# The recurrence's token shift on VectorE alone, and another room for half of the read-out

## The chip, the cores and the metric

The kernel runs on one core of one Trainium2 chip. The metric is the time of one execution on the device, in microseconds (us). The core has five engines with a queue of instructions each: TensorE (PE; its weight loads are listed apart as PEld), VectorE (DVE), ScalarE (ACT), GpSimd (POOL) and SyncE (SP), which here issues all transfers. An engine takes its own instructions in order; engines wait for each other through semaphores. Matmuls write to banks of PSUM (128 partitions by 512 floats here); VectorE and ScalarE read these banks, and a bank can be written anew only when its readers are through.

## What is computed

A decoder layer on 1024 tokens of width 1024, in float32. A normalised input is multiplied by one wide matrix; its columns feed a windowed attention, an RWKV-7 recurrence with 8 heads of 64, and two gates. Their merged output goes through a projection, an MLP and an embedding gate. The part that matters here is the token shift ahead of the recurrence, and the recurrence's read-out:

```python
z = z + (token_shift(z) - z) * mu          # token_shift: z of the token before, 0 for the first
r, k, v, xw, xa, xg = jnp.split(z, RWKV_SPLITS, axis=-1)
...
_, y = lax.scan(step, state0, seq)
y = (y - mean) * lax.rsqrt(var + RWKV_GN_EPS)
y = y.reshape(B, S, RWKV_WIDTH) * ln_w.astype(f32) + ln_b.astype(f32)
...
y = (y + bonus.reshape(B, S, RWKV_WIDTH)) * g.astype(f32)
```

So each shifted tile is (1 - mu) times the product, plus mu times the product one token earlier.

## The kernel before, in words

Tokens lie along the free axis of the tiles of the recurrence, features along the partitions. The wide product is made in column blocks of 128 features, each in two halves of 512 tokens. One half is 24 matmuls into one bank: 8 slices of the width, and for each three products (`L310`, `L312`, `L314`), since a float32 operand is held as a rounded high part and a low remainder. The weights of a block are loaded by `wload`, rounded by ScalarE (`wh`) and the remainder made by GpSimd (`wl`, 128x1024).

The recurrence is worked in four units of 128 features (two heads). For each unit w, `add_rkv` makes the blocks of r, k and v; when a half is in its bank, `shift_half` takes it out of it and applies the token shift. While the recurrence runs, the dense halves alternate between two banks, z0 and z1 (`zbank`), so a half's first matmul waits until the half before the last has been taken out.

`shift_half` existed in two forms. The early form, used once for the small tiles `xw` and `xg`: ScalarE writes (1 - mu) times the bank to the tile (`omu` is its scale), and VectorE adds mu times the bank, shifted by one column, in one scalar_tensor_tensor; the first column of the second half comes from a kept column, `edge`. The other form, used for r, k and v (24 halves): ScalarE reads the bank twice, once for (1 - mu) times it, and once for mu times it into a tile `part`; GpSimd adds `part`, shifted, to the tile. `part` stands in the rooms of the tag `gst`, of which there are two; the same rooms stage the gate columns on their way to DRAM.

Per unit follow `elementwise` (decays, normalised keys; VectorE operations of 128x1024 elements: `AR`, `kk`, `BK`), `invert` (31 pairs of short VectorE steps, `pt` and `xy`), `fold_v` and `fold` (small matmuls), `scan` (14 steps, a small matmul `q` and a VectorE operation each), `read_out` (`y`), and `post`. `post` runs twice per unit, for the two token halves b = 0 and 1, one after the other: ScalarE squares the bank (`sq`) and copies it (`yc`), PE sums and transposes, VectorE makes `yc`, adds `bv` and multiplies into `og`, which is stored. Both halves used the one room `yc`, so the second half's copy had to wait for the first half's last reader.

The order of all this is set when the program is built. The class `Order` keeps an estimated clock; chains of the recurrence are recorded as they come due by it, and dense matmuls (the projections' blocks, among them the 16 gate blocks) fill PE's time between them. Each engine's estimated end moves with each operation recorded on it, and the steps of the inverse are put into VectorE's estimated idle time. So an operation that goes to another engine moves many others by some places. On the chip each engine then follows its recorded order.

Line numbers in the profile: most operations of VectorE, ScalarE and GpSimd go through one helper and are recorded under `L118` (held-back ones under `L115`), DMAs under `L137`; matmuls under `L293`, transposes under `L301`, and dense matmuls under `L310` to `L314`. So groups are told apart by the tiles' names.

## Time and profile before

| | us |
|---|---|
| median of 3 runs | 1758.35 |
| the three runs | 1755.95, 1758.35, 1758.49 |
| the profiled execution's own time | 1760.41 |
| its span, first to last instruction | 1758.6 |

The profile is of one execution. Of its span, roughly the first 50 us prepare the input, the recurrence lies between 50 and 525 us, attention up to about 830, merging and projection up to about 1050, and the MLP and the end take the rest. A row of the timeline gives start and duration in us, the engine, the line, the operation, output and inputs, shapes, and in brackets the idle time of that engine just before, with what ended it. A granted clock of 0.50 means that TensorE ran at half its full rate in that stretch.

### The profile page before, as it was taken

How to read it: one execution, taken by the hardware profiler on the slowest of the kernel's cores; microseconds unless marked ns; L12 is line 12 of the kernel's file. 1: busy time of each engine (PE TensorE's matmuls, PEld its weight loads, DVE VectorE, ACT ScalarE, POOL GpSimd, SP SyncE). 2: the span in 40 equal slices, each digit the busy share in tenths (PEclk: the TensorE clock that was granted, in tenths of full speed). 3: DMA queues.
4: the chain of work that ended last, by engine and by line, in shares of the span. 5: the costliest groups of instructions: out<-in, count | busy, mean ns of one | idle time of the engine just before them, and what ended most of it. 6: DMA issues, size and time to landing. Idle time of an engine off the chain costs nothing.

```text
span 1758.6 us, 26456 instructions
## 1 busy us (share of the span) xinstructions
PE 1731.2 (98%) x10132; PEld 1411.8 (80%) x10132; DVE 1102.0 (63%) x1878; ACT 751.6 (43%) x1377; POOL 639.5 (36%) x441
## 2 busy tenths in 40 slices
PE   9999999999999999999999998999999999999998
PEld 8787878887887877777888876888888888888887
DVE  6278876757635233444746652767788788787643
ACT  5833523342335343462534555333433443343354
POOL 1233111211212322322230346656656756752311
PEclk9999999999999999999999999999999999999999
DMA  4620121212342222232633386364464664567611
GB/s 164 213 96 28 58 90 56 80 36 81 113 141 92 67 60 61 84 138 103 212 108 126 108 326 248 124 224 160 145 234 179 204 227 163 203 223 271 224 49 48
DMA packets 99970, 244.78 MB, mean 139 GB/s; under 512 B 11394, under 2 KB 11778, under 8 KB 99331
## 3 DMA queue, kind: packets, MB, share of 16 engines
q1 hardware_dynamic: 99842, 243.08, 40.0%
q8 instruction: 80, 1.31, 0.3%
q14 instruction: 48, 0.39, 0.1%
HBM read 169.24 MB, written 67.11 MB: 134 GB/s over the span
## 4 chain that ended last, share of the span: by engine, by line
PE 82%; DVE 8%; ACT 4%; POOL 2%; issue 2%; DMA 2%; SPq 0%; DVEq 0%; ACTq 0%; POOLq 0%
PE z L314 15%; PE z L312 15%; PE z L310 15%; PE bk L310 8%; PE bk L314 8%; PE bk L312 8%; DVE tot L118 2%; DVE xy L118 1%; PE tp L301 1%; PE sc L293 1%; PE A L293 1%; PE y L293 1%; PE wr L293 1%; PE pt L301 1%; PE fq L293 1%
## 5 line engine op out<-in xcount | busy, mean ns | idle before, releaser
L310 PE MATMUL z<-uh,wh 128*128 128x512 f32 (+1 forms) x800 | 313.8, 392 | 2.5 <-ACT uh L118 1.3
L312 PE MATMUL z<-ul,wh 128*128 128x512 f32 (+1 forms) x800 | 314.3, 393 | 1.3 <-DVE ul L118 1.3
L314 PE MATMUL z<-uh,wl 128*128 128x512 f32 (+1 forms) x800 | 314.0, 392 | 1.2 <-POOL wl L118 1.1
L118 POOL TENSOR_TENSOR wl<-wr,wh 128x1024 fp32r<-128x1024 f32 (+1 forms) x56 | 133.8, 2390 | 469.4 <-ACT wh L118 461.7
L118 DVE TENSOR_TENSOR tot<-tot,bk 128x512 f32<-128x512 f32 x333 | 219.8, 683 | 82.2 <-PE bk L314 82.1
L310 PEld LDWEIGHTS z<-uh,wh 128*128 128x128 f32 x800 | 151.8, 190 | 33.6 <-issue 3.4
L314 PEld LDWEIGHTS z<-uh,wl 128*128 128x128 f32 x800 | 151.7, 190 | 32.8 <-issue 3.9
L312 PEld LDWEIGHTS z<-ul,wh 128*128 128x128 f32 x800 | 151.8, 190 | 32.0 <-issue 3.7
L118 ACT ACTIVATE wh<-wr 128x1024 fp32r<-128x1024 f32 (+2 forms) x94 | 81.1, 863 | 117.0 <-PE z L312 69.8
L118 ACT ACTIVATE hr<-hr 128x512 f32<-128x512 f32 x96 | 60.7, 632 | 133.4 <-DVE hr L118 131.9
L310 PE MATMUL bk<-duo 128*128 128x512 f32 x224 | 88.4, 395 | 0.4
L118 ACT ACTIVATE duo<-sum 128x512 fp32r<-128x512 f32 x64 | 39.7, 627 | 113.1 <-DVE sum L118 100.6
L312 PE MATMUL bk<-duo 128*128 128x512 f32 x224 | 87.7, 392 | 0.0
L314 PE MATMUL bk<-duo 128*128 128x512 f32 x224 | 87.6, 391 | 0.0
L310 PE MATMUL bk<-ws,duo 128*128 128x512 f32 x224 | 87.1, 389 | 0.0
L312 PE MATMUL bk<-ws,duo 128*128 128x512 f32 x224 | 87.1, 389 | 0.0
L314 PE MATMUL bk<-ws,duo 128*128 128x512 f32 x224 | 87.1, 389 | 0.0
L310 PE MATMUL z<-f,wh 128*128 128x512 f32 x212 | 83.1, 392 | 3.5 <-ACT pa L118 3.5
L314 PE MATMUL z<-f,wh 128*128 128x512 f32 x212 | 83.4, 393 | 1.3 <-POOL wh L118 1.3
L118 POOL TENSOR_TENSOR wh<-wr,wh 128x512 fp32r<-128x512 f32 x38 | 54.5, 1436 | 81.3 <-ACT wh L118 81.3
L312 PE MATMUL z<-f,wh 128*128 128x512 f32 x212 | 83.0, 391 | 0.0
L118 DVE TENSOR_TENSOR hr<-hr,z 128x512 f32<-128x512 f32 x80 | 54.6, 682 | 23.4 <-PE z L314 23.3
(372 smaller groups left out, 4052.4 us busy)
## 6 DMA issues: line engine op xcount, KB each, us to landing
wr<-in_wz_dram SPq DMA_DIRECT2D x48, 512.0 KB, 3.8
w2r<-in_w_ff_dram SPq DMA_DIRECT2D x34, 512.0 KB, 4.6
bs<-duo SPq DMA_DIRECT2D x32, 512.0 KB, 4.9
duo<-bs SPq DMA_DIRECT2D x32, 512.0 KB, 4.2
wr<-in_wff_dram SPq DMA_DIRECT2D x56, 256.0 KB, 3.6
hr<-p1scr SPq DMA_DIRECT2D x48, 256.0 KB, 4.0
xt<-in_x_dram SPq DMA_DIRECT2D x16, 512.0 KB, 3.8
gscr<-gst SPq DMA_DIRECT2D x32, 256.0 KB, 2.2
```

Of the source, the lines that this page charges most:

```text
L118: return f(*a, **kw)
L293: PE.matmul(out_, a, b, start=start, stop=stop)
L301: PE.transpose(out_, a, ident if idn is None else idn)
L310: PE.matmul(ps, ah, bh, start=start and i == 0, stop=False, skip_group_check=not start)
L312: PE.matmul(ps, ah, bl, start=False, stop=False, skip_group_check=not start)
L314: PE.matmul(ps, al, bh, start=False, stop=i == n - 1, skip_group_check=not start)
```

## The change

`shift_half` keeps the early form only and uses it for r, k and v too. The tile `part`, its 24 ScalarE copies and all of GpSimd's adds are gone; VectorE reads the bank a second time instead. In `post`, the second half's `yc` moves to one of the two `gst` rooms that `part` no longer uses.

```diff
-    def shift_half(dst, ps, h, mu, om, edge, early=False):
+    def shift_half(dst, ps, h, mu, om, edge):
         lo, hi = h * 512, h * 512 + 512
         S.activation(dst[:, lo:hi], ps, AF.Copy, scale=om)
-        if early:
-            if h == 0:
-                V.tensor_copy(edge, ps[:, 511:512])
-            else:
-                V.scalar_tensor_tensor(dst[:, lo:lo + 1], edge, mu, dst[:, lo:lo + 1], op0=OP.mult, op1=OP.add)
-            V.scalar_tensor_tensor(dst[:, lo + 1:hi], ps[:, 0:511], mu, dst[:, lo + 1:hi],
-                                   op0=OP.mult, op1=OP.add)
-            return
-        part = rtile([128, 512], "part", "gst")
-        S.activation(part, ps, AF.Copy, scale=mu)
         if h == 0:
-            G.tensor_copy(edge, part[:, 511:512])
+            V.tensor_copy(edge, ps[:, 511:512])
         else:
-            G.tensor_tensor(dst[:, lo:lo + 1], edge, dst[:, lo:lo + 1], OP.add)
-        G.tensor_tensor(dst[:, lo + 1:hi], part[:, 0:511], dst[:, lo + 1:hi], OP.add)
+            V.scalar_tensor_tensor(dst[:, lo:lo + 1], edge, mu, dst[:, lo:lo + 1], op0=OP.mult, op1=OP.add)
+        V.scalar_tensor_tensor(dst[:, lo + 1:hi], ps[:, 0:511], mu, dst[:, lo + 1:hi], op0=OP.mult, op1=OP.add)
...
-            shift_half(t, ps, h, pr[:, c], omu[:, c], edges[:, n:n + 1], True)
+            shift_half(t, ps, h, pr[:, c], omu[:, c], edges[:, n:n + 1])
...
-        yc = rtile([128, 512], "yc", "yc")
+        yc = rtile([128, 512], "yc", ("yc", "gst")[b])
```

Since the order is recorded by estimates, the instructions of all engines move up to the first projection. VectorE's queue in the first unit's `elementwise`, after the change (each row one instruction, or several alike; `v<-z` is the new operation on a half of v in its bank `z`):

```order
L118 TENSOR_TENSOR BK<-a,En 128x16x64
L118 COPY edge<-z 128x1
L118 SCALAR_TENSOR_TENSOR v<-z,pr,v 128x511
L115 COPY wc<-Ep 128x16
L115 TENSOR_TENSOR AR<-r,Ep 128x1024
L118 SCALAR_TENSOR_TENSOR kk<-k,pr,bc 128x512 x2
L118 SCALAR_TENSOR_TENSOR AR<-kk,Ep 128x16x63
L118 TENSOR_SCALAR AR<-kk 128x16
L118 TENSOR_TENSOR BK<-BK,En 128x16x64
L118 SCALAR_TENSOR_TENSOR v<-edge,pr,v 128x1
L118 SCALAR_TENSOR_TENSOR v<-z,pr,v 128x511
L118 TENSOR_TENSOR BK<-BK,kk 128x16x64
```

Before, the rows without `z` and `edge` stood there in the same order, and GpSimd made v beside them. The second half of v now stands behind the whole block of six operations from `AR<-r,Ep` to `BK<-BK,En`. In the second unit these rows stand in the same order, with steps of the inverse (`pt`, `xy`) ahead of and behind them.

ScalarE's queue in the second unit, from the exponentials to the gate columns, before:

```order
L118 ACTIVATE En<-Ep 128x1024
L118 ACTIVATE v<-z,omu 128x512
L118 ACTIVATE part<-z,pr 128x512
L115 ACTIVATE Ep<-Ep 128x1024
L118 ACTIVATE v<-z,omu 128x512
L118 ACTIVATE part<-z,pr 128x512
L118 ACTIVATE wh<-wr 128x1024
L118 ACTIVATE gst<-z 128x512 x2
```

and in the same place after the change:

```order
L118 ACTIVATE En<-Ep 128x1024
L118 ACTIVATE wh<-wr 128x1024
L118 ACTIVATE v<-z,omu 128x512
L115 ACTIVATE Ep<-Ep 128x1024
L118 ACTIVATE v<-z,omu 128x512
L118 ACTIVATE wh<-wr 128x1024
L118 ACTIVATE gst<-z 128x512 x2
```

Both `part` copies are gone, and the rounding `wh` of a block's weights, which stood ahead of the reciprocal norms, now stands between `En` and the first half of v.

## The prediction

> **What bounds the kernel now.** First the page: the span, and the busy time by engine.

> ```profile
> span 1758.6 us, 26456 instructions
> PE 1731.2 (98%) x10132; PEld 1411.8 (80%) x10132; DVE 1102.0 (63%) x1878; ACT 751.6 (43%) x1377; POOL 639.5 (36%) x441
> ```

> TensorE is busy for 98% of the span. It executes the same matmuls after the change, so nothing is won by work taken from ScalarE or GpSimd as such; only two things can move the end: the idle time of PE, 27.4 us in all, and the time it runs at a lower granted clock. So next come PE's own waits, by what ended them (total, times, longest; the rows that touch the changed lines).

> ```profile
> PE q L293 <- DVE AR L118: 1.9, 2, 1.0
> PE z L310 <- ACT part L118: 1.2, 1, 1.2
> PE A L293 <- ACT yc L118: 1.0, 1, 1.0
> ```

> The tiles of the change appear there twice, once each: the scaled copy `part` costs PE 1.2 us, the read-out tile `yc` 1.0 us. Third, the granted clock. The stretches below are (duration, PE busy, PEld, DVE, ACT, then PEclk); I chose the borders at the clock's own changes.

> ```profile
> 262.33:265.75 3.42, 2.70 (x65) 2.58 (x66) 3.33 (x5) 0.98 (x2) 0.00 (x0) 1.00 0.30 106
> 265.75:272.57 6.82, 6.82 (x44) 5.22 (x41) 3.42 (x3) 1.85 (x3) 3.39 (x3) 0.50 0.18 65
> 351.08:354.49 3.41, 3.41 (x17) 2.27 (x16) 3.41 (x2) 2.11 (x2) 0.00 (x0) 0.50 0.83 217
> 361.32:364.73 3.41, 3.41 (x49) 3.32 (x47) 1.39 (x3) 3.36 (x6) 0.00 (x0) 1.00 0.02 5
> 364.73:368.15 3.42, 3.42 (x12) 2.60 (x9) 1.25 (x2) 3.38 (x8) 0.00 (x0) 0.50 0.00 0
> ```

> Three times in the recurrence the clock is halved, for 6.82, 3.41 and 3.42 us, which costs half of that: 3.4, 1.7 and 1.7 us, 6.8 us together. The first halving follows the stretch in which PE waits for `yc`. [...] So I count the halvings as something that the order of small matmuls can bring or take, and not as a fixed cost.

> **The change part by part.** Every token-shift half had two reads of the bank by ScalarE and an add by GpSimd. The view of the tile `part` and, for the form that replaces it, of `xw` and `edges`, where the kernel already has it (instructions, min/median/max in ns):

> ```profile
> L118 ACT ACTIVATE part<-z,pr x24: 673/682/697, 55.2 to 373.6; 128x512 f32<-128x512 f32 x24
> L118 POOL TENSOR_TENSOR r<-part,r x8: 1086/1090/1306, 57.6 to 334.5; 128x511 f32<-128x511 f32 x8
> L118 DVE SCALAR_TENSOR_TENSOR xw<-z,pr,xw x2: 737/740/742, 37.3 to 44.6; 128x511 f32<-128x511 f32 x2
> L118 DVE COPY edges<-z x2: 147/148/150, 37.2 to 38.3; 128x1 f32<-128x1 f32 x2
> L118 DVE SCALAR_TENSOR_TENSOR xg<-edges,pr,xg x1: 220/220/220, 48.4 to 48.4; 128x1 f32<-128x1 f32 x1
> ```

> ScalarE loses 24 x 0.682 = 16.4 us, GpSimd 24 x 1.09 = 26.2 us and its small edge operations. VectorE gains 24 x 0.740 + 12 x 0.148 + 12 x 0.220 = 22.2 us between 54 and 375 us. None of these is a term by itself. What counts is that **the bank is now given back by VectorE**, behind whatever stands in VectorE's queue. Two banks alternate here, so a bank must be free again when the next half's 24 matmuls are through. These rows of ScalarE time that: each copy starts when a half ends.

> ```profile
> 149.41 0.50 PE L310 MATMUL z<-uh,wh 128*128 128x512 f32 x1 [1.21 <-ACT part L118]
> 155.30 0.60 ACT L118 ACTIVATE gst<-z 128x512 f32<-128x512 f32 x1 [2.89 <-PE z L314]
> 160.72 0.60 ACT L118 ACTIVATE gst<-z 128x512 f32<-128x512 f32 x1 [4.82 <-PE z L314]
> ```

> A half takes 160.72 - 155.30 = 5.42 us. That is the cover. For most of the 24 it is enough, since VectorE has no block of long operations ahead: for r and k the new operations stand between the short steps of the inverse, and I cost them at nothing. If the cover were gone, each would cost its 0.96 us.

> *First unit, v, second half.* Here the new operations stand behind a block. VectorE's timeline of that block before the change, and GpSimd's split beside it:

> ```profile
> 90.90 1.40 DVE L118 SCALAR_TENSOR_TENSOR kk<-k,pr,bc 128x512 f32<-128x512 f32 x2
> 92.33 1.97 DVE L118 SCALAR_TENSOR_TENSOR AR<-kk,Ep 128x1008 f32<-128x1008 f32 x1
> 94.23 2.37 DVE L118 TENSOR_SCALAR AR<-kk 128x16 f32<-128x16 f32 x1
> 96.50 1.21 DVE L118 TENSOR_TENSOR BK<-BK,En 128x1024 f32<-128x1024 f32 x1
> 93.20 3.36 POOL L118 TENSOR_TENSOR wl<-wr,wh 128x1024 fp32r<-128x1024 f32 x1
> 90.80 0.69 ACT L118 ACTIVATE v<-z,omu 128x512 f32<-128x512 f32 x1 [1.33 <-PE z L314]
> 96.32 0.60 ACT L118 ACTIVATE gst<-z 128x512 f32<-128x512 f32 x1 [3.30 <-PE z L314]
> ```

> The v half ended at 90.8, the next at 96.3, and there PE wants the bank back. PE has the same matmuls ahead of that point in the new order. VectorE is through with `BK<-BK,En` at 96.50 + 1.21 = 97.7; then 0.22 + 0.74, less two overlaps of 0.1 such as between the rows at 94.23 and 96.50, give 98.5. That is a wait of 98.5 - 96.3 = **2.2 us**. If GpSimd's split did not stand in the way, the 128x16 operation would take 0.17 us (a row of the second unit, below) instead of 2.37, and the wait would be nothing. The bounds are 0 and 2.2; I take 2.2, because the split follows the same `wh` in the new order and the rows are those of this very place.

> *Second unit, v.* VectorE's block in that place:

> ```profile
> 151.92 1.21 DVE L115 TENSOR_TENSOR AR<-r,Ep 128x1024 f32<-128x1024 f32 x1
> 153.05 1.39 DVE L118 SCALAR_TENSOR_TENSOR kk<-k,pr,bc 128x512 f32<-128x512 f32 x2
> 154.48 3.17 DVE L118 SCALAR_TENSOR_TENSOR AR<-kk,Ep 128x1008 f32<-128x1008 f32 x1
> 157.57 0.17 DVE L118 TENSOR_SCALAR AR<-kk 128x16 f32<-128x16 f32 x1
> 157.65 1.22 DVE L118 TENSOR_TENSOR BK<-BK,En 128x1024 f32<-128x1024 f32 x1
> 148.11 0.67 ACT L118 ACTIVATE v<-z,omu 128x512 f32<-128x512 f32 x1
> 151.34 1.07 ACT L118 ACTIVATE wh<-wr 128x1024 fp32r<-128x1024 f32 x1
> 144.08 0.17 DVE L118 TENSOR_SCALAR rn<-hs 128x16 f32<-128x16 f32 x1
> 249.09 1.86 DVE L118 SCALAR_TENSOR_TENSOR AR<-kk,Ep 128x1008 f32<-128x1008 f32 x1
> ```

> For the first half PE waited until 149.41 behind `part`. In the new order a weight's rounding `wh` (1.07 us) stands ahead of that half's ScalarE copy, and 0.148 + 0.740 of VectorE behind it, so by the old clock times the release would be 148.11 + 1.07 + 0.67 + 0.89 = 150.7, 1.3 us later. Against that, the normalisation that everything here hangs on reads its bank at 144.08, behind a backlog of the inverse's steps, and the new order puts fewer of them in front. Bounds: 1.2 us won to 1.3 us lost. I take **0**, the middle, as no row decides.

> For the second half VectorE has 1.21 + 1.39 + 1.86 + 0.17 + 1.22 + 0.22 + 0.74 = 6.8 us, from the first half's release to the second's, against a cover of 5.42 us: a wait of 1.4 us; with the slowed 3.17 instead of 1.86, 2.7 us. I take **1.4**, because a split that used to be beside this operation has moved to the front of the first half.

> *The read-out.* `yc` of the second half gets one of the two `gst` rooms. Before, it waited for the first half's last reader:

> ```profile
> 263.05 0.49 PE L293 MATMUL A<-AR,BK 64*128 64x128 f32 x4 [1.05 <-ACT yc L118]
> ```

> That wait goes: **-1.05**. Next in line for the same matmul is ScalarE's square, which stands just ahead of the copy. What the room costs: a gate's copy two places behind `yc` has to wait for the read-out's last product. In the new order one read-out (first unit) is followed by the next-but-one gate copy only after the fold's copies, another (third unit) after two copies of the inverse. Nothing to 2 us, on ScalarE; I take 0, since PE's other bank covers 5.42 us of it.

> VectorE's added 22.2 us push each unit's inverse back; the new order lets PE do dense work there, taken from the gate columns (the first fold starts 46 dense matmuls later). That costs nothing as long as dense work is left, and 25 dense matmuls, 5.6 us, still stand behind the last attention product (73 before). The scan's steps may wait for VectorE as in the first waits row (two, 1.9 us); bounds -1.9 to +3.8 (four halves of 0.96 us fall among scan steps); I take 0.

> **Sum** against the profiled execution's own 1760.41 us: +2.2 + 0 + 1.4 - 1.05 = +2.55. The profiled execution is 2.06 us above the median 1758.35, so the forecast is 1758.35 + 2.55 = **1760.9 us**, no difference that a measurement tells: I call 0.2%, 3.5 us, the limit of that.

> **The rivals.**

> *Faster.* The yc wait goes and with it the half clock behind it: -1.05 - 3.4. VectorE also gets back what GpSimd's adds took from it.

> ```profile
> 124.56 1.31 POOL L118 TENSOR_TENSOR r<-part,r 128x511 f32<-128x511 f32 x1 [0.32 <-ACT part L118]
> 124.56 0.35 DVE L118 TENSOR_TENSOR pt<-xy,Mp 64x192 f32<-64x192 f32 x1
> 124.94 1.13 DVE L118 TENSOR_TENSOR xy<-xy,pt 64x192 f32<-64x192 f32 x1
> 246.37 3.51 POOL L118 TENSOR_TENSOR wl<-wr,wh 128x1024 fp32r<-128x1024 f32 x1 [14.72 <-ACT wh L118]
> 247.65 1.41 DVE L118 SCALAR_TENSOR_TENSOR kk<-k,pr,bc 128x512 f32<-128x512 f32 x2
> ```

> Beside such an add a step of 192 elements took 1.13 us instead of its neighbour's 0.35. With the adds gone the banks come back in time, and the 1.21 us goes as well: -5.7, 1752.7 us. For it: the halving follows the yc wait directly. Against it: the splits of the weights remain, and they are the longer GpSimd operations. [...] Chance 0.23.

> *Slower.* The mechanism is the bank release: PE's first matmul of the gate half that follows v stands and waits. With both waits at their long end and the first half not won back it is 2.2 + 1.3 + 2.7 - 1.05 = 5.15, and a wait of this length in a stretch makes the next one half as fast, as 262.33:265.75 did with 2.70 us busy of 3.42: 1.7 us once: +6.85, 1765.2 us. It decides from the point where VectorE's release comes more than 5.42 us after the half's end. A third fold with less dense work between its small matmuls, as the new order has it, adds another 1.7. Chance 0.32.

> *No effect at all.* ScalarE and GpSimd were covered, VectorE's operations are, too, and only yc's 1.05 goes: 1757.3 us, inside the same 0.2%. Chance 0.12, and 0.33 for my sum.

> **How the numbers follow.** The two cases within 0.2% hold 0.45, faster 0.23, slower 0.32. The range reaches from the faster rival to the slower one with another halving: 1752 to 1768.

> **What would show it.** Right: PE waits of 1 to 3 us ended by "DVE v" at about 97 and 155 us, no wait for `part` or `yc`; the DVE busy time up by some 15 to 22 us, POOL down by about 30. Wrong: no wait ended by a shifted tile at all; or a wait for `r` or `k`; or another count of half-clock stretches than three in the recurrence, which moves the time by 1.7 us each; or ScalarE waiting for a `gst` room.

## The result and the profile after

The changed kernel takes 1753.6 us (median of 20 runs, 1751.6 to 1757.8), the kernel before 1758.42 us beside it (20 runs, 1755.0 to 1763.85). The ratio is 0.9971, 95% interval 0.9962 to 0.998: **faster by 0.3%**, 5 us. The prediction was 1760.9 us, no difference; the measured time lies in its range of 1752 to 1768, near the end that the faster rival gave. A second comparison on another chip gave 0.9957 (0.9941 to 0.9973).

The page of the changed kernel, span and busy times:

```profile
span 1753.7 us, 26435 instructions
PE 1727.1 (98%) x10132; PEld 1409.0 (80%) x10132; DVE 1108.6 (63%) x1926; ACT 736.9 (42%) x1353; POOL 606.0 (35%) x393
```

The span is 4.9 us shorter, and PE is busy 4.1 us less with the same 10132 matmuls: its idle time went from 27.4 to 26.6 us only. Less the time that the whole span lost at half clock (10.9 us before, 5.8 us after), PE's busy time is 1720.4 us before and 1721.3 us after, so what it gained is clock. PE's waits, the rows that answer to those shown of before (total, times, longest):

```profile
PE z L310 <- DVE v L118: 3.2, 2, 2.7
PE q L293 <- DVE AR L118: 1.7, 4, 0.6
```

The waits for `part` (1.2 us) and `yc` (1.0 us) are gone, and two waits for `v` from VectorE have come, 3.2 us together. By these rows alone the kernel would be a microsecond slower. So I look at the stretches around the clock (duration, PE busy, PEld, DVE, ACT, POOL, granted clock); the first row is nearly the whole recurrence:

```profile
56.00:525.00 469.00, 462.88 (x4038) 380.54 (x4037) 321.85 (x615) 168.58 (x253) 78.41 (x41) 1.00 0.26 91
148.00:151.42 3.42, 0.72 (x5) 0.33 (x4) 3.39 (x7) 1.63 (x2) 1.34 (x2) 1.00 0.00 0
151.42:154.83 3.41, 3.41 (x9) 2.67 (x10) 3.41 (x4) 0.00 (x0) 1.27 (x1) 0.50 0.00 0
274.30:277.71 3.41, 3.41 (x80) 2.93 (x80) 3.31 (x4) 0.59 (x1) 0.00 (x0) 1.00 0.34 132
```

The same row of the kernel before:

```profile
56.00:525.00 469.00, 461.70 (x4018) 378.80 (x4018) 314.23 (x571) 183.98 (x278) 110.32 (x88) 0.99 0.27 92
```

In the recurrence there is now one half clock, 3.41 us at 151.4 us, behind the longer wait for `v`; before there were three, 13.66 us in all. That is 5.1 us of full-clock time (13.66 - 3.41, halved), as much as the whole difference of the two spans. The fold in the second unit (274.30: 80 matmuls, most of them 32x32) is at full clock; before, the stretch that held it (262.33, 65 matmuls, with the `yc` wait) was followed by 6.82 us at half clock.

This is one profile of each kernel, and a second one of each, taken for the experiments, divides the gain otherwise: PE's idle time in the whole span falls from 27.3 to 24.8 us, and the time lost at half clock only from 7.6 to 6.2 us. Over all executions on that chip the mean granted clock is 0.9950 before and 0.9967 after, which is 3.0 us of a difference of 7 us. So the clock is one part of the gain, and PE's waits are the other.

The two waits for `v`, in the timeline of the changed kernel:

```profile
92.71 3.32 POOL L118 TENSOR_TENSOR wl<-wr,wh 128x1024 fp32r<-128x1024 f32 x1 [8.96 <-ACT wh L118]
93.70 2.35 DVE L118 SCALAR_TENSOR_TENSOR v<-edge,pr,v 128x1 f32<-128x1 f32 x1
95.97 0.73 DVE L118 SCALAR_TENSOR_TENSOR v<-z,pr,v 128x511 f32<-128x511 f32 x1
96.85 0.47 PE L310 MATMUL z<-uh,wh 128*128 128x512 f32 x1 [0.46 <-DVE v L118]
...
145.87 2.39 POOL L118 TENSOR_TENSOR wl<-wr,wh 128x1024 fp32r<-128x1024 f32 x1 [14.44 <-ACT wh L118]
145.88 2.65 DVE L118 TENSOR_TENSOR xy<-xy,pt 64x247 f32<-64x247 f32 x1
148.46 1.21 DVE L118 TENSOR_TENSOR BK<-a,En 128x1024 f32<-128x1024 f32 x1
149.59 0.39 DVE L118 TENSOR_TENSOR pt<-xy,Mp 64x240 f32<-64x240 f32 x1
150.02 0.40 DVE L118 TENSOR_TENSOR xy<-xy,pt 64x240 f32<-64x240 f32 x1
150.41 0.73 DVE L118 SCALAR_TENSOR_TENSOR v<-z,pr,v 128x511 f32<-128x511 f32 x1
151.29 0.66 PE L310 MATMUL z<-uh,wh 128*128 128x512 f32 x1 [2.70 <-DVE v L118]
```

In the first unit a one-element add took 2.35 us beside GpSimd's split, but VectorE's block had begun early enough: 0.46 us of wait. In the second unit a step of the inverse took 2.65 us beside a split (its neighbours take 0.4), and behind it stood 1.21 + 0.39 + 0.40 us of other work before the first half of `v` could be taken out: 2.70 us. The large operation itself, fed from the bank, took 0.73 us in both places, in the second unit beside a split that began at 150.34 us.

### The profile page after: what moved, and what is told of

The parts are those of the page before. It is cut to its first block, busy times and chain, and to the rows that moved or that the text cites. A ratio compares the mean times of both kernels' runs of the same rounds, so it can differ in the third digit from the quotient of the medians.

```text
span 1753.7 us, 26435 instructions
## 1 busy us (share of the span) xinstructions
PE 1727.1 (98%) x10132; PEld 1409.0 (80%) x10132; DVE 1108.6 (63%) x1926; ACT 736.9 (42%) x1353; POOL 606.0 (35%) x393
## 3 DMA queue, kind: packets, MB, share of 16 engines
q8 instruction: 80, 1.31, 0.3%
## 4 chain that ended last, share of the span: by engine, by line
PE 80%; DVE 7%; ACT 4%; DMA 4%; issue 2%; POOL 2%; SPq 1%; DVEq 0%; ACTq 0%; POOLq 0%
PE z L310 15%; PE z L314 15%; PE z L312 15%; PE bk L310 8%; PE bk L314 8%; PE bk L312 8%; PE tp L301 1%; PE sc L293 1%; PE A L293 1%; PE po L293 1%; PE pt L301 1%; PE wr L293 1%; PE fq L293 1%; DVE duo L118 1%; POOL wl L118 1%
## 5 line engine op out<-in xcount | busy, mean ns | idle before, releaser
L118 POOL TENSOR_TENSOR wl<-wr,wh 128x1024 fp32r<-128x1024 f32 (+1 forms) x56 | 133.3, 2382 | 589.8 <-ACT wh L118 584.4
L310 PE MATMUL z<-uh,wh 128*128 128x512 f32 (+1 forms) x800 | 313.4, 392 | 4.0 <-DVE v L118 3.2
L314 PE MATMUL z<-uh,wl 128*128 128x512 f32 (+1 forms) x800 | 312.9, 391 | 0.7 <-POOL wl L118 0.7
L118 DVE TENSOR_TENSOR tot<-tot,bk 128x512 f32<-128x512 f32 x333 | 219.6, 681 | 82.3 <-PE bk L314 82.1
L310 PEld LDWEIGHTS z<-uh,wh 128*128 128x128 f32 x800 | 151.0, 189 | 36.0 <-issue 4.9
L314 PEld LDWEIGHTS z<-uh,wl 128*128 128x128 f32 x800 | 151.1, 189 | 31.8 <-issue 3.7
L118 ACT ACTIVATE wh<-wr 128x1024 fp32r<-128x1024 f32 (+2 forms) x94 | 81.0, 862 | 119.5 <-PE z L312 65.9
L118 ACT ACTIVATE hr<-hr 128x512 f32<-128x512 f32 x96 | 60.7, 632 | 134.8 <-DVE hr L118 133.3
L310 PE MATMUL bk<-duo 128*128 128x512 f32 x224 | 88.4, 395 | 0.3
L314 PE MATMUL bk<-duo 128*128 128x512 f32 x224 | 87.5, 391 | 0.0
L314 PE MATMUL bk<-ws,duo 128*128 128x512 f32 x224 | 87.1, 389 | 0.0
L310 PE MATMUL bk<-ws,duo 128*128 128x512 f32 x224 | 87.1, 389 | 0.0
L118 ACT ACTIVATE duo<-sum 128x512 fp32r<-128x512 f32 x64 | 39.7, 628 | 112.4 <-DVE sum L118 100.5
L310 PE MATMUL z<-f,wh 128*128 128x512 f32 x212 | 83.1, 392 | 3.5 <-ACT pa L118 3.5
L314 PE MATMUL z<-f,wh 128*128 128x512 f32 x212 | 83.4, 393 | 1.3 <-POOL wh L118 1.3
L118 POOL TENSOR_TENSOR wh<-wr,wh 128x512 fp32r<-128x512 f32 x38 | 54.5, 1437 | 81.2 <-ACT wh L118 81.2
L118 DVE TENSOR_TENSOR hr<-hr,z 128x512 f32<-128x512 f32 x80 | 54.5, 681 | 23.4 <-PE z L314 23.3
```

The lines of the kernel that those rows point to most:

```text
L118: return f(*a, **kw)
L310: PE.matmul(ps, ah, bh, start=start and i == 0, stop=False, skip_group_check=not start)
L314: PE.matmul(ps, al, bh, start=False, stop=i == n - 1, skip_group_check=not start)
```

## The experiments

Three theories stood against each other: the gain is in the *order* of the matmuls and the clock that it is granted (A), in the *work* and the waits that it brought (B: ScalarE's and GpSimd's parts of the shift no longer in anyone's way), or in the new *room* alone (C). Since the planner sets the order by the work that it is told of, the work and the order can be parted: an inserted engine that does nothing takes the calls that only the planner is to see, and the real operations are issued beside it.

### The room alone

The kernel before with one line changed; every compute engine has the same instructions in the same order.

```diff
-        yc = rtile([128, 512], "yc", "yc")
+        yc = rtile([128, 512], "yc", ("yc", "gst")[b])
```

> Only the room of yc changes: the second half's read-out gets one of the gst rooms, the shift stays on ScalarE and GpSimd, and every compute engine has the same instructions in the same order as before. Theory A (the gain of the changed kernel is clock: fewer half-clock stretches in the recurrence, brought by another order of the small matmuls): the 1.05 us wait of PE for yc goes; the half clock at 265.7 us, which followed that wait, may go with it or stay, since no order has changed: between -1 us (1757.4) and -4.5 us (1753.9). Theory B (the gain is PE's waits for part and yc, 1.2 + 1.05 us): -1.0 us, 1757.4, three half-clock stretches in the recurrence as before. Theory C (the whole gain sits in the room alone): 0.997, about 1753.6.

Measured: 0.9983 (0.9973 to 0.9993), -3.0 us. More than the wait alone (theory B) and less than the whole (theory C). In its profile the wait for `yc` is gone and so is the half clock behind it; one of 3.41 us at 352 us is left. The recurrence:

```profile
56.00:525.00 469.00, 461.81 (x4044) 379.24 (x4044) 320.25 (x582) 187.45 (x285) 113.46 (x89) 1.00 0.28 93
```

### The changed kernel with the old room

```diff
-        yc = rtile([128, 512], "yc", ("yc", "gst")[b])
+        yc = rtile([128, 512], "yc", "yc")
```

> The changed kernel with yc back in its single room; the order on every engine is that of the changed kernel. Theory A (order of the matmuls sets the half-clock stretches): one half-clock stretch in the recurrence instead of three, as in the changed kernel, or one more if the yc wait is back and brings it: 0.997 to 0.998, 1753.6 to 1756.3. Theory B (waits): the yc wait is back, 1754.7. Theory C (the room): 1758.4, as before.

Measured: 0.9984 (0.9973 to 0.9994); the changed kernel has 0.9971 and 0.9957. The order on every engine is that of the changed kernel, so the stretch at 274 us can be laid beside the one above. First the timeline of PE with the old room, then the stretches:

```profile
274.35 0.39 PE L310 MATMUL z<-uh,wh 128*128 128x512 f32 x1
274.66 0.48 PE L293 MATMUL A<-AR,BK 64*128 64x128 f32 x2
276.19 1.16 PE L293 MATMUL A<-AR,BK 64*128 64x128 f32 x14 [1.04 <-ACT yc L118]
277.28 2.57 PE L293 MATMUL tq<-TN,TM 32*32 32x32 f32 x64
279.78 0.80 PE L312 MATMUL z<-ul,wh 128*128 128x512 f32 x1
```

```profile
275.44:278.85 3.41, 2.66 (x63) 2.54 (x64) 3.32 (x5) 0.94 (x2) 0.00 (x0) 1.00 0.27 100
278.85:285.68 6.83, 6.83 (x46) 5.29 (x42) 3.49 (x3) 1.90 (x3) 3.40 (x3) 0.50 0.22 68
```

With the old room the wait of 1.04 us is back in the stretch that holds the fold, and behind it 6.83 us at half clock, 3.4 us lost. So the room takes away 1.05 us of wait *and* the half clock behind it, in either order.

The same matmuls in the changed kernel:

```profile
274.34 0.39 PE L310 MATMUL z<-uh,wh 128*128 128x512 f32 x1
274.66 1.16 PE L293 MATMUL A<-AR,BK 64*128 64x128 f32 x16
275.75 2.21 PE L293 MATMUL tq<-TN,TM 32*32 32x32 f32 x64
277.89 0.50 PE L312 MATMUL z<-ul,wh 128*128 128x512 f32 x1
```

From the end of the last dense matmul (`z`) to the start of the next it is 5.0 us with the wait and 3.2 us without it. A whole stretch of 3.41 us, as at 275.44, can stand without a dense matmul only in the first. That is how a wait of 1 us can bring a half clock; it is read from these rows and was not tried by itself.

### The new work in the old order, and the old work in the new one

The first has VectorE's shift and the new room, but the planner is told of the old work; TensorE's matmuls stand exactly as in the kernel before. The second has ScalarE's and GpSimd's shift and the new room, but TensorE's matmuls exactly as in the changed kernel.

```diff
+        S.eng, G.eng = NoOp(), NoOp()
         part = rtile([128, 512], "part", "gst")
         S.activation(part, ps, AF.Copy, scale=mu)
...
+        S.eng, G.eng = nc.scalar, nc.gpsimd
...
+        nc.vector.scalar_tensor_tensor(dst[:, lo + 1:hi], ps[:, 0:511], mu, dst[:, lo + 1:hi], op0=OP.mult, op1=OP.add)
```

```diff
+            V.eng = NoOp()
...
         V.scalar_tensor_tensor(dst[:, lo + 1:hi], ps[:, 0:511], mu, dst[:, lo + 1:hi], op0=OP.mult, op1=OP.add)
+        V.eng = nc.vector
...
+        part = rtile([128, 512], "part", "gst")
+        nc.scalar.activation(part, ps, AF.Copy, scale=mu)
...
+        nc.gpsimd.tensor_tensor(dst[:, lo + 1:hi], part[:, 0:511], dst[:, lo + 1:hi], OP.add)
```

> VectorE makes the second term, and yc has the new room, but the order is that of the kernel before: TensorE has the same matmuls in the same order as before, and VectorE's added operations stand where the shift stood. Theory A (order): no gain, 1758.4 or up to 2.2 us more from the bank waits; the half clocks at 351 and 364.7 us, which are far from any shift, are still there. Theory B (work: ScalarE's copy of the bank and GpSimd's adds in VectorE's way): 0.997, 1753.6.

> ScalarE and GpSimd make the second term as before, and yc has the new room, but TensorE's matmuls, VectorE's and ScalarE's remaining operations stand in the order of the changed kernel. Theory A (order): 0.997, 1753.6, less the two bank waits behind VectorE (3.2 us together) plus a wait for part of about 1 us: 1750 to 1754, with at most one half-clock stretch in the recurrence. Theory B (work): 1.000, 1757 to 1758.4, three half-clock stretches.

Measured: new work, old order 1.0011 (1.0 to 1.0022); old work, new order 0.9959 (0.9944 to 0.9975). Theory B falls on both, and theory C falls with the room alone, which gives only 3.0 of the 5 us. With the same room and the old order, VectorE's work costs 1.0011 - 0.9983 = 0.0028, 4.9 us, and the intervals are apart. Its waits for `v` (`L510` is the shift there) and the recurrence:

```profile
PE z L316 <- DVE v L510: 4.9, 3, 3.8
...
56.00:525.00 469.00, 459.63 (x4000) 376.04 (x3999) 322.01 (x616) 168.73 (x252) 75.63 (x40) 0.99 0.27 91
```

and of the old work in the new order:

```profile
56.00:525.00 469.00, 465.12 (x4053) 382.26 (x4051) 313.26 (x566) 182.35 (x277) 113.16 (x89) 1.00 0.27 91
```

PE's idle time in that window is 469.00 - 459.63 = 9.4 us in the one and 3.9 us in the other. With the room alone (old work, old order) it is 7.2 us: the new order by itself saves 3.3 us of waits, among them the 1.2 us for `part` and two of 0.6 us before `hs`. From the room alone (0.9983) to the old work in the new order (0.9959) it is 4.2 us in the time; their intervals touch, but each of the five runs of the new order (up to 1754.86 us) is below each of the twelve of the old one (from 1755.66), on the same chip. The mean granted clock of the executions is 0.9960 with the room alone and 0.9958 here, so the clock has no part in it. As far as these runs show, theory A is right that the order counts, but what the order gains is waits, and the gain in clock comes with the room.

### Each kernel once more, and v by the old path

Both kernels unchanged, for a second profile; and the changed kernel with a part of the work taken back: r and k by VectorE, v by ScalarE and GpSimd, TensorE's order kept by the inserted engine as above.

```diff
     def evac(h, ps, nm=nm, pc=pc):
...
-                           d["e" + nm])
+                           d["e" + nm], nm != "v")
```

> The kernel before, unchanged, for a second profile and for the clock of its executions beside the others on one chip. If a half-clock stretch belongs to the place of the program (the yc wait and the 6.83 us half clock behind it at about 265 us), it is there again; the stretches at 351 and 364.7 us as well if the order of the small matmuls sets them. If the stretches are scattered by chance, the second profile has them at other places. Ratio 1.000 within the interval; mean clock of the executions 0.9946 as in the last comparison (9.5 us lost).

> The changed kernel, unchanged, for a second profile. By place: the wait of 2.7 us for v at 151 us and a 3.4 us half clock behind it again, none at 265 to 280 us, since no yc wait is there. Ratio 0.997; mean clock 0.9964 (6.3 us lost). If the order saves PE's idle time, the span without the lost clock is also some 2 us below that of the kernel before.

> The changed kernel, with r and k shifted by VectorE as in it, but v again by ScalarE and GpSimd; TensorE's matmuls in exactly the changed kernel's order, yc in its new room. If the price of VectorE's work is the two bank waits for v and the half clock behind the longer one, as the prediction had it, both go: 3.2 + 1.7 us less than the changed kernel, less a wait for part of up to 1.2 us that may come: 0.9950 to 0.9960 of the kernel before, as the run with the old work in the new order (0.9959), and no half clock at 151 us. If the price lies in r and k as well (VectorE later by 16 operations of 0.74 us), it stays at 0.997.

Measured: 0.9998 (0.9986 to 1.001), 0.9957 (0.9941 to 0.9973), and **0.9929** (0.9912 to 0.9945) for v by the old path, 1748.4 us, the best of all; no run of it (1745.99 to 1748.86) reaches the changed kernel's on the same chip (1751.71 to 1754.06). It is 4.1 us below it, and below the 0.9950 to 0.9960 that was expected; the two waits and the half clock behind the longer came to 3.2 + 1.7. Neither is in its profile, and the recurrence has no half clock at all:

```profile
56.00:525.00 469.00, 466.31 (x4070) 384.37 (x4069) 317.83 (x601) 175.34 (x264) 94.17 (x57) 1.00 0.27 93
```

The second profile of the kernel before repeats the half clock behind the `yc` wait, half as long, and not the one at 351 us (one at 362.66 us answers to that at 364.73):

```profile
263.67:267.08 3.41, 3.32 (x79) 3.16 (x79) 3.35 (x4) 0.63 (x2) 0.00 (x0) 1.00 0.45 154
267.08:270.49 3.41, 3.41 (x15) 2.47 (x17) 1.57 (x1) 1.65 (x2) 1.65 (x1) 0.50 0.23 81
```

The `yc` wait ends at 263.76 us here, as the first of these stretches begins: what stands in the stretch ahead of the half clock is the fold, and the wait has kept the dense matmuls out of it (none from 262.31 to 266.99). So some half clocks belong to a place, and some come in one execution and not in the next. The changed kernel's second profile repeats its one, at 151.7 us.

### Other orders of the same work

Is the new order better because the planner knows of the new work, or was it a lucky one? Two of the planner's estimates were moved, each with the old work (and the new room) and with the new work.

```diff
-HOP = 0.15
+HOP = 0.18
```

```diff
-LEAD, SPARE, LAG, HELD = 0.4, 0.5, 0.4, 2.5
+LEAD, SPARE, LAG, HELD = 0.4, 0.5, 0.5, 2.5
```

> The old work with the new room, and the planner's price for handing a tile to another engine changed from 0.15 to 0.18 us, which gives a third order of the matmuls. It has nothing to do with the shift. If the order of the changed kernel is better by chance, this one may fall on either side of the old order with the same room (0.9983), by up to 3 us; if the changed kernel's order is better because the planner was told the new work, this one stays at 0.998, PE's idle time in the recurrence at 5 us and not 2.

> The changed kernel with the planner's price for handing a tile on at 0.18 us: the partner of the run with the old work, the new room and the same price (1.0007). If the planner's knowledge of the new work gives a better order in any case, this one is again 0.002 to 0.004 below its partner: 0.997 to 0.999, PE idle 2 to 3 us less in the recurrence (bank waits for v not counted). If the changed kernel's order was a lucky one among several, it lies on either side of its partner.

> The old work with the new room, and the planner's allowed lag at 0.5 us in place of 0.4: a fourth order that has nothing to do with the shift. By chance alone: anywhere from 0.996 to 1.001. If the order of the old work is bad in any case: 0.998 to 1.001, PE idle some 5 us in the recurrence, a wait for part of about 1 us.

> The changed kernel with the allowed lag at 0.5 us, the partner of the run before. If telling the planner of the new work is what makes the order better: 0.002 to 0.004 below its partner. By chance: on either side. A wait for v of 2 us or more is followed by a half clock of 3.4 us or more within 5 us, as in the four profiles that have one; without such a wait there is none at that place.

The last run is the version that somebody would write after the run above: v by the old path, and the planner told so.

> r and k shifted by VectorE, v by ScalarE and GpSimd, yc in its new room, and the planner told so: the order is its own. If what counts is that no bank is given back by VectorE behind its block for v: no wait for v, no half clock at 145 to 155 us, and 0.993 to 0.996. If the order of the changed kernel carried most of the gain of the run with v by the old path (0.9929), this one lands near the old order's level, 0.998.

Measured: old work 1.0007 (0.9995 to 1.0019) and 0.9961 (0.9949 to 0.9974); new work 1.0026 (1.0013 to 1.0038) and 1.0043 (1.003 to 1.0057); v by the old path in its own order 0.9985 (0.9977 to 0.9994), with no wait for `v` but not the gain either. With the old work and the new room, then, order alone spans 0.9959 to 1.0007, over 8 us, with the same instructions. The new work in its planner's own order gives 0.9971, 1.0026 and 1.0043: the changed kernel's order was a good draw, not a consequence of the shift. Both slower ones have the 2.7 us wait for `v` with a half clock behind it at 152 us, and another one, of 6.83 and 10.24 us, behind the second unit's fold. No `yc` wait stands ahead of that fold in either, but other waits do (0.47 us for `UV`, 0.72 us for `kk`), so the `yc` wait is one way to a half clock there and not the only one. The spread is wider than expected: the other hop with the old work lies 4.2 us above the room alone, and 3 was the bound.

All kernels side by side. *Idle* is 469 us less PE's busy time between 56 and 525 us of one profile, *half clock* half of the time at clock 0.50 in that window:

| kernel | ratio | idle | half clock | sum |
|---|---|---|---|---|
| new shift, v by the old path, new order | 0.9929 | 2.7 | 0.0 | 2.7 |
| old work, new order, new room | 0.9959 | 3.9 | 1.7 | 5.6 |
| old work, other lag | 0.9961 | 6.2 | 0.0 | 6.2 |
| changed kernel (two profiles) | 0.9971, 0.9957 | 6.1, 6.0 | 1.7, 1.7 | 7.8, 7.7 |
| room alone | 0.9983 | 7.2 | 1.7 | 8.9 |
| changed kernel, old room | 0.9984 | 7.3 | 5.1 | 12.4 |
| v by the old path, own order | 0.9985 | 5.3 | 0.0 | 5.3 |
| before (two profiles) | 1, 0.9998 | 7.3, 7.7 | 6.8, 3.4 | 14.1, 11.1 |
| old work, other hop | 1.0007 | 6.8 | 1.7 | 8.5 |
| new work, old order | 1.0011 | 9.4 | 6.8 | 16.2 |
| new work, other hop | 1.0026 | 9.1 | 5.1 | 14.2 |
| new work, other lag | 1.0043 | 8.1 | 6.8 | 14.9 |

The sum of one profile and the measured ratio go together (correlation 0.84 over the 14 profiles; 1.1 us of time for 1 us of sum). Where they don't (old work with the other hop, v by the old path in its own order), the profile shows half clocks outside the recurrence as well, at 533 and 762 us, and at 545 us; others have such, too. *Idle* alone goes with the ratio as well as the sum does (0.85), the half clock alone less (0.75). Over the whole span the account closes: PE's busy time less the time lost at half clock is 1718.9 to 1721.9 us in all 14 profiles, while their spans reach from 1746.6 to 1764.8 us. What makes the kernels differ is PE's idle time and its clock, and little else.

## Why the prediction was wrong, step by step

Two terms failed that the sum had at nothing: the half clock behind the `yc` wait, and the order of the matmuls. By the runs the room is worth -3.0 us where the sum had -1.05, and the order -4.2 where it had 0; VectorE's work, in the sum at +3.6, came to +2.1 in the new order (0.9971 against 0.9959, not clear of noise) and to +4.9 in the old one. In the new order that is -3.0 - 4.2 + 2.1 = -5.1 us, where the sum was +2.55.

- **What bounds the kernel**: right. Only PE's idle time and its clock moved the end. ScalarE lost 14.7 us and GpSimd 33.5 us of work, and none of it shows in the time.
- **The halvings**: the first step that failed. The prediction saw that one halving more or less is worth 1.7 us, saw that the first one follows the `yc` wait, had one in its rows behind a stretch in which PE is busy throughout (361.32), and then counted them "not as a fixed cost", at nothing in the sum. No run shows that nothing: the one behind `yc` goes with the wait. It is there in all three profiles with the `yc` wait (6.83, 3.41 and 6.83 us); with the wait gone and the order kept, in either order, it is gone. The mean granted clock of all executions says the same: 0.9946 before and 0.9960 with the room alone, 0.9950 and 0.9964 in the new order without and with the room (these two are from different comparisons, and the kernel before has 0.9946, 0.9950 and 0.9956 in three of them); 0.0014 of 1758 us is 2.5 us.
- **The yc wait, -1.05**: right in place and size, but the term should have been about -3: measured -3.0 us with the room alone (by its interval -1.2 to -4.7).
- **The order**: the second step that failed, and the larger. It was priced at nothing wherever no row decided (the scan's steps, the inverse, the second unit's first half). The runs give the new order -4.2 us, from 0.9983 to 0.9959, by shorter waits of PE and not by clock. This could have been bounded only by the spread that orders show, and no row of the profile of before had its sign: the other two orders came out on both sides.
- **First unit, v, second half, +2.2**: came, at 0.46 us. A one-element operation met the split in place of the 128x16 one, and took 2.35 us in place of 0.22, but VectorE's block stood earlier. The 128x16 operation at 94.23 had taken 2.37 us beside a split in the kernel before. The 24 large new operations took 0.73 to 0.75 us each, the one beside the second unit's split among them (0.73).
- **Second unit, v**: the first half, priced at 0 with 1.3 as the upper bound, was the late one: a wait of 2.70 us against 1.21 before, +1.5. The row at 144.08 was to decide it, by a backlog of the inverse; it was the split beside one of those steps that did. The second half, priced at +1.4, waited for nothing. The bank terms together were forecast at +3.6 and came to 0.46 + 1.49 = +1.95, and the half clock behind the longer wait, which only the slower rival had, adds 1.7.
- **The work altogether**: forecast slower. In the old order that is what it is, by 4.9 us; in the new one 0.9959 against 0.9971 and 0.9957 can't be told apart. The part that costs is v: with v by the old path and the order kept the kernel is 4.1 us faster.
- **r and k at nothing; the scan at nothing; the room's cost on ScalarE at nothing**: right. PE never waits for a shifted r or k; its waits for the scan's `AR` were 1.9 us and are 1.7.
- **The faster rival** had 1752.7 us by the wait and the half clock behind it (-1.05 - 3.4) and the 1.2 us of `part`. Its first two terms are what the room does; its third, that the banks come back in time, did not happen: that the time came out near it is luck, as the order, which it doesn't name, paid for the waits. Its own reason, that VectorE gets time back from GpSimd, fits: VectorE's new operations add 24 us of busy time (three times 5.9 for the large ones, 3.0 + 0.9 + 0.8 + 1.8 for the small), and the page shows only 6.6 more (the room alone, with unchanged work, shows 3.3 less).
- **What would show it**: waits of "DVE v" at 97 (0.46 us and not 1 to 3) and at 151 in place of 155 us, none for `part` or `yc`, POOL down by 33.5, but DVE up by 6.6 and not by 15 to 22; and the sign named for a wrong prediction, another count of half clocks than three in the recurrence, is the one that came.

Open: which waits make the changed kernel's order better than the others was read from one profile each, not tried one by one. How the `yc` wait brings its half clock was read from the rows of PE, not tried. That the old work in the new order (0.9959) is slower than v alone by the old path (0.9929) also has no tested cause; the two were compared on different chips, and the first has half clocks at 463 and 1044 us that the other lacks.

## What to carry to other kernels

Where TensorE bounds the kernel, price a short wait with the half clock behind it: a wait of 1 us among small matmuls cost 3 us here, as measured, and one of 2.7 us cost 4.4 by its profile (2.7 + 1.7). When an edit changes what a planner is told, measure the edit in the old order and the old work in the new order before crediting the edit: here the work lost in the old order, and the new order won. Keep the instruction that gives a bank back off the engine that has a block of long operations at that moment, even where it is the cheaper engine in sum: here that was worth 4.1 us with the order kept, though the same version in its planner's own order came out at 0.9985.

## What the runs showed of the clock

A stretch with PE busy from end to end can be followed by a half clock all the same. One of the runs with another order has this, PE's timeline and then the stretches:

```profile
351.55 1.84 PE L293 MATMUL hs<-cs,kk 128*128 128x2 f32 x16
353.31 2.21 PE L293 MATMUL tr<-TQ,TM 32*32 32x32 f32 x64
355.45 0.79 PE L314 MATMUL z<-uh,wl 128*128 128x512 f32 x1
```

```profile
352.05:355.46 3.41, 3.41 (x77) 3.35 (x77) 2.37 (x4) 2.12 (x5) 2.35 (x1) 1.00 0.00 0
355.46:358.87 3.41, 3.41 (x10) 2.73 (x9) 1.65 (x2) 3.36 (x6) 0.00 (x0) 0.50 0.00 0
```

PE is busy for all of 3.41 us with 77 matmuls, all small but the last, and is at half clock for the next 3.41. I gave each matmul its streamed columns, weighted by the share of the 128x128 array that its weights fill, and summed them by window of the grid, over the 14 profiles between 40 and 1745 us; a window of dense matmuls has about 7,700 (15 of 512 columns). Of 36 windows at full clock below 2,000, that is below four dense matmuls, 29 were followed by a half clock; of 221 between 2,000 and 3,200, 10; of 6,677 above 3,200, none. In the first profiles of the two kernels alone it is 6 of 7 (the seventh is the fold at 274.30, at 1,924), none of 29 and none of 954. (The counts move by two or three with the way in which a matmul across a border is shared out.) The weighting and the borders are my own; they fit these profiles, and no run was made to test them. By this count the wait of 2.7 us for `v` leaves its window at 1,100 (148.00 us in the changed kernel) to 2,900, by where the grid cuts it, and a window falls below 2,000 with a fold of 64 matmuls of 32x32 (128 in all) with fewer than about four dense ones (512 each) beside it. The fold at 275.75 took 2.21 us, less than a window, so whether one falls into one window or two is up to the phase: that fits half clocks that come in one execution of a kernel and not in the next, and the spread of one kernel's executions (29 of the kernel before on one chip: 1757.04 to 1764.52 us, mean granted clock 0.997 to 0.992). An order that puts dense matmuls among the 64 of each fold was not tried.
